# Hybrid decoder layer: key transposes one projection earlier, score matmuls of a head grouped by shape

## The chip, the cores and the metric

The kernel runs on one core of one Trainium2 chip. The metric is the device time of one execution in microseconds; less is better. The time before is the median of three executions.

## The reference

One layer on a sequence of 512 tokens of width 1024, all in float32: a layer norm, one large projection, two causal token mixers in parallel, an output projection with a second layer norm, and then a mixer that picks 16 of 16384 experts per head for every token. The change lies in the first token mixer, a gated linear recurrence that is computed in chunks (8 heads, key and value width 128):

```python
def hgrn2_mixer(q, f_logit, i, g, lb, norm_g):
    f = lb + (1.0 - lb) * jax.nn.sigmoid(f_logit.astype(f32))
    k = 1.0 - f
    logf = jnp.log(f)
    ...
    bh = jnp.cumsum(heads(logf, HG_DK), axis=3)
    q_dec = qh * jnp.exp(bh)
    k_inv = kh * jnp.exp(-bh)
    scores = jnp.where(causal, jnp.einsum('bhncd,bhnsd->bhncs', q_dec, k_inv), 0.0)
    o_intra = jnp.einsum('bhncs,bhnse->bhnce', scores, vh)
    k_end = kh * jnp.exp(b_last - bh)
    d_state = jnp.einsum('bhncd,bhnce->nbhde', k_end, vh)
    ...
    _, s_in = lax.scan(step, s0, (chunk_decay, d_state))
    o_inter = jnp.einsum('bhncd,nbhde->bhnce', q_dec, s_in)
```

So a head needs scores (decayed queries against keys), a product of the scores with the values, and a product of transposed decayed keys with the values that moves the state from one block of tokens to the next.

## The kernel before, in words

Tokens lie in four blocks of 128. Every projection is a feature tile, `proj` (line 374): 8 slices of the width times 3 matmuls of 128x128 on 128x512 (lines 123 to 125; each float32 weight is split into a high and a low part), that is 24 matmuls into one of two PSUM tiles `fp`. Its weight tile is loaded by DMA (`wraw`), its high part is cast on ACT (`wh`, line 118) and its low part subtracted on POOL (`wl`, line 119), three to four tiles ahead.

The list `slots` (lines 557 to 561) holds 44 projections. The first 24 are three for each head: the forget gate (`f_tile`), the query (`q_tile`) and the output gate (`g_tile`). Behind each projection the loop at line 562 issues parts of earlier heads. With h the head, and slot 3h the one of its `f_tile`:

- `att1(h)` behind slot 3h+3, the f projection of the next head. It transposes the decayed keys `kb` of the head (line 447, tile `k` in the trace, since the buffer is reused) into the PSUM tile `pk`, copies that to `ktok` on ACT (line 449), and computes the scores into the PSUM tile `psc`. For each of the four blocks there are four matmuls: one 128x128 (line 453), one with 64 columns of weights for the later half block against the earlier (line 455), and two with 32 columns at column positions 0 and 64 (line 459). They overwrite parts of what the first wrote, and DVE copies the result under the causal mask to `sc` (line 463).
- `att2(h)` behind slot 3h+4, the q projection of the next head. Three matmuls of `ktok` with the values (line 474, tile `pd`), and from them the states `st` on DVE (lines 475 and 477).
- `att3(h)` behind slot 3h+5, the g projection of the next head. Scores times values and queries times state (lines 487 and 489, tile `po`), squares and a norm on ACT (lines 494 to 496), a product on DVE (line 498).
- `att4(h)` behind slot 3h+7. Transposes of the result (line 506, tile `pr`), gate and split (line 508 on).

TensorE (PE) runs in the order in which the program is written. In this part the order of ACT, DVE, POOL and SyncE comes from the framework's scheduler. A PE instruction that waits for another engine holds all PE work behind it. The temporary tiles (`f`, `k`, `kinv`, `half`, `q`, `ktok`, `o`) share 15 buffers in turn, and the PSUM tiles `pk`, `psc`, `pd`, `po` and `pr` share six banks in turn.

After the mixers come the branch projection, the output projection and the norm, the expert queries with their top-16 lists, and a long phase over all 128 tiles of expert keys and values (lines 1046 to 1094).

Of the kernel before, what the change touches and what calls it, by code (L numbers as in the profile page):

```python
# [20 lines left out]
NB = 4  # L21
# [30 lines left out]
def hybrid_block(ctx, tc, ins, out, dbg=None):  # L52
# [14 lines left out]
    def bank(name="bank"):  # L67
        return psw.tile([128, 512], FT, name=name, tag="bank")
# [167 lines left out]
    with ExitStack() as pa:  # L236
# [6 lines left out]
        def tmp(name="tmp", dt=FT):  # L243
            return t2.tile([128, S], dt, name=name, tag="t2")
# [134 lines left out]
        hd = [dict() for _ in range(H)]  # L379
# [60 lines left out]
        def head(h):  # L440
            return vtok[h // 4], slice((h % 4) * 128, (h % 4 + 1) * 128)

        def att1(h):
            x = hd[h]
            pk = bank("pk")
            for blk in range(NB):
                nc.tensor.transpose(pk[:, blk * 128:(blk + 1) * 128], x["kb"][:, blk * 128:(blk + 1) * 128], ident)
            ktok = tmp("ktok")
            nc.scalar.copy(ktok, pk)
            psc_ = bank("psc")  # L450
            for blk in range(NB):
                sl = slice(blk * 128, (blk + 1) * 128)
                nc.tensor.matmul(psc_[:, sl], x["kinv"][:, sl], x["q"][:, sl], start=True, stop=True,
                                 skip_group_check=True)
                nc.tensor.matmul(psc_[0:64, blk * 128 + 64:(blk + 1) * 128], x["half"][:, 0, blk, :], x["half"][:, 1, blk, :],
                                 start=True, stop=True, skip_group_check=True)
                for j in (0, 2):
                    s = blk * 128 + j * CH
                    nc.tensor.matmul(psc_[j * CH:(j + 1) * CH, s + CH:s + 2 * CH], x["be"][:, s:s + CH],
                                     x["q"][:, s + CH:s + 2 * CH], start=True, stop=True, skip_group_check=True,  # L460
                                     tile_position=(0, j * CH))
            sc = scT[h % 2]
            nc.vector.copy_predicated(sc, smask[:, None, :].to_broadcast([128, NB, 128]),
                                      psc_.rearrange("p (b c) -> p b c", b=NB))
            x.update(ktok=ktok, sc=sc)

        def att2(h):
            x = hd[h]
# [92 lines left out]
                  (pool_tile, 3)] + [(gb_tile, t) for t in range(4, 8)] + [(ga_tile, t) for t in range(8)]  # L561
        for n, (fn, arg) in enumerate(slots):
            fn(arg)
            for lag, att in ((7, att4), (5, att3), (4, att2), (3, att1)):
                h, r = divmod(n - lag, 3)
                if r == 0 and 0 <= h < H:
                    att(h)
# [565 lines left out]
def build(nc, arrays, dbg=None):  # L1133
    ins = {k: nc.dram_tensor(f"in_{k}_dram", v.shape, mybir.dt.from_np(v.dtype), kind="ExternalInput").ap()
           for k, v in arrays.items()}
    out = nc.dram_tensor("out_0_dram", (S, D), FT, kind="ExternalOutput").ap()
    d = {k: nc.dram_tensor(f"dbg_{k}", shp, FT, kind="ExternalOutput").ap() for k, shp in (dbg or {}).items()}
    with tile.TileContext(nc) as tc:
        hybrid_block(tc, ins, out, d)
# [11 lines left out]
```

## Time and profile before

| | us |
|---|---|
| median of 3 executions (lowest to highest) | 1815.38 (1810.57 to 1819.29) |
| the profiled execution, own time | 1821.71 |
| its span in the trace | 1820.0 |
| PE busy in the span | 1759.8 |
| DVE busy | 1302.0 |
| ACT busy | 748.4 |
| POOL busy | 642.0 |

The trace shows one execution with every instruction. A float32 matmul stands in it as two records, here called passes; a transpose has one. "Busy" on PE is modelled from starts and shapes, so the distance from one start to the next tells more of its pace than the length of a record does. PEld are the weight loads, which can run beside matmuls. A time in square brackets is idle time of the engine just before the instruction, with the instruction that ended it.

### The profile page before, as it was taken

What the parts mean: (1) busy time and instruction counts of PE and PEld (TensorE: products, weight loads), DVE (VectorE), ACT (ScalarE), POOL (GpSimd) and SP (SyncE); (2) the same over time, 40 slices, a digit from 0 to 9 for tenths busy, and PEclk for the clock granted to TensorE, in tenths of its full rate; (3) what the DMA queues carried; (4) which work ended last, traced back from release to release, by engine and by line L of the source; (5) the groups of instructions that cost most, each with busy time, mean ns of one, the idle gap of its engine ahead of it and who ended that gap; (6) DMA issues with size and microseconds to landing.
All of it is one profiled execution on the core that took longest, in us unless ns stands there. A gap on an engine that the chain in (4) does not pass through costs nothing.

```text
span 1820.0 us, 25277 instructions
## 1 busy us (share of the span) xinstructions
PE 1759.8 (97%) x9677; PEld 1539.9 (85%) x9677; DVE 1302.0 (72%) x2332; ACT 748.4 (41%) x1052; POOL 642.0 (35%) x421
## 2 busy tenths in 40 slices
PE   7999999999999999999999999999999999999997
PEld 5777787888788998888988888888878888888886
DVE  6455444234589869999846887887867887878887
ACT  3567754332332355655653343323333332333332
POOL 3532323344345540000012543453433443444450
PEclk9999999999999999999999999999999999999999
DMA  4322222342233335565688999899998999899983
GB/s 145 117 69 70 60 69 87 104 139 93 77 96 115 106 109 174 197 232 192 239 291 277 367 335 375 320 317 360 315 325 291 339 336 323 312 338 325 328 304 105
DMA packets 159694, 399.10 MB, mean 219 GB/s; under 512 B 12882, under 2 KB 75858, under 8 KB 156372
## 3 DMA queue, kind: packets, MB, share of 16 engines
q1 hardware_dynamic: 115220, 253.02, 41.5%
q0 software_dynamic: 36864, 134.23, 20.5%
q10 hardware_dynamic: 7488, 10.23, 1.5%
q8 instruction: 76, 1.25, 0.3%
q14 instruction: 46, 0.38, 0.1%
HBM read 359.94 MB, written 37.49 MB: 218 GB/s over the span
## 4 chain that ended last, share of the span: by engine, by line
PE 77%; DVE 9%; DMA 5%; issue 2%; ACT 2%; ACTq 0%; DVEq 0%; SPq 0%
PE fp L123 14%; PE fp L124 14%; PE fp L125 14%; PE yacc L124 8%; PE yacc L125 8%; PE yacc L123 8%; DMA wraw<-in_v_tab_dram 4%; PE ple L841 3%; DVE A L876 2%; DVE wl L220 2%; PE pG L890 2%; DVE oh L870 2%; DMA wraw<-in_u_tab_t_dram 1%; PE sc L785 1%; PE acc L125 1%
## 5 line engine op out<-in xcount | busy, mean ns | idle before, releaser
L123 PE MATMUL fp<-othi,wh 128*128 128x384 f32 (+1 forms) x1216 | 429.2, 353 | 0.3 <-ACT othi L136 0.3
L125 PE MATMUL fp<-othi,wl 128*128 128x384 f32 (+1 forms) x1216 | 420.7, 346 | 6.2 <-DVE wl L220 6.2
L219 ACT CAST wh<-wraw 128x1024 fp32r<-128x1024 f32 x280 | 294.3, 1052 | 308.1 <-DMA wraw<-in_v_tab_dram 203.9
L124 PE MATMUL fp<-otlo,wh 128*128 128x384 f32 (+1 forms) x1216 | 419.6, 345 | 0.2 <-DVE otlo L137 0.2
L220 DVE TENSOR_TENSOR wl<-wraw,wh 128x1024 fp32r<-128x1024 f32 x246 | 300.4, 1224 | 156.1 <-ACT wh L219 155.6
L967 POOL DMA_INDIRECT rows<-in_u_tab_dram,eidx x128 | 179.6, 1403 | 494.4 <-DVE oh L870 248.3
L123 PE MATMUL yacc<-wh,ah 128*128 128x512 f32 x768 | 301.0, 392 | 6.6 <-ACT wh L219 6.6
L124 PE MATMUL yacc<-wl,ah 128*128 128x512 f32 x768 | 302.6, 394 | 4.0 <-DVE wl L220 4.0
L125 PE MATMUL yacc<-wh,al 128*128 128x512 f32 x768 | 302.0, 393 | 0.0
L967 POOL DMA_INDIRECT rows<-in_v_tab_dram,eidx x128 | 186.9, 1461 | 231.1 <-DVE hres L981 193.3
L119 POOL TENSOR_TENSOR wl<-wraw,wh 128x1024 fp32r<-128x1024 f32 x68 | 167.8, 2471 | 277.3 <-ACT wh L118 277.3
L125 PEld LDWEIGHTS fp<-othi,wl 128*128 128x128 f32 x1216 | 229.4, 189 | 14.4 <-DVE wl L220 6.9
L124 PEld LDWEIGHTS fp<-otlo,wh 128*128 128x128 f32 x1216 | 229.8, 189 | 10.3 <-DVE otlo L137 0.5
L123 PEld LDWEIGHTS fp<-othi,wh 128*128 128x128 f32 x1216 | 229.6, 189 | 10.3 <-ACT othi L136 0.5
L627 ACT ACTIVATE ge<-fp 128x384 f32<-128x384 f32 x128 | 62.9, 492 | 352.8 <-PE fp L125 352.8
L123 PEld LDWEIGHTS yacc<-wh,ah 128*128 128x128 f32 x768 | 145.2, 189 | 36.8 <-ACT wh L219 8.1
L124 PEld LDWEIGHTS yacc<-wl,ah 128*128 128x128 f32 x768 | 145.2, 189 | 35.2 <-DVE wl L220 6.2
L125 PEld LDWEIGHTS yacc<-wh,al 128*128 128x128 f32 x768 | 145.2, 189 | 30.7 <-DVE al L119 0.3
L981 DVE SCALAR_TENSOR_TENSOR hres<-rows,ggate,hres 128x1024 f32<-128x1024 f32 x128 | 164.1, 1282 | 2.4
L978 DVE SCALAR_TENSOR_TENSOR rows<-rows,hg 128x1024 f32<-128x1024 f32 x128 | 151.1, 1219 | 0.7 <-DMA rows<-in_u_tab_dram,eidx 0.7
L123 PE MATMUL fp<-xthi,wh 128*128 128x512 f32 x352 | 142.4, 405 | 1.5 <-DVE q L426 1.5
L118 ACT CAST wh<-wraw 128x1024 fp32r<-128x1024 f32 x68 | 71.1, 1048 | 163.9 <-issue 100.6
(245 smaller groups left out, 2519.5 us busy)
## 6 DMA issues: line engine op xcount, KB each, us to landing
wraw<-in_u_tab_t_dram SPq DMA_DIRECT2D x128, 512.0 KB, 4.9
wraw<-in_v_tab_dram SPq DMA_DIRECT2D x128, 512.0 KB, 7.0
Gd<-stg SPq DMA_DIRECT2D x24, 1024.0 KB, 6.3
gt<-Gd SPq DMA_DIRECT2D x16, 1536.0 KB, 15.5
wraw<-in_w_in_dram SPq DMA_DIRECT2D x44, 512.0 KB, 3.5
Hs<-ge ACTq DMA_DIRECT2D x52, 192.0 KB, 2.7
ge<-Hs SPq DMA_DIRECT2D x52, 192.0 KB, 7.5
wraw<-in_w_query_dram SPq DMA_DIRECT2D x16, 512.0 KB, 3.4
```

Source lines behind the costliest of these rows:

```text
L118: nc.scalar.copy(hi, src)
L119: lo_eng.tensor_sub(lo, src, hi.bitcast(FT))
L123: nc.tensor.matmul(o, a[0], b[0], start=start, stop=False)
L124: nc.tensor.matmul(o, a[0], b[1], start=False, stop=False)
L125: nc.tensor.matmul(o, a[1], b[0], start=False, stop=stop)
L219: f(hi, raw)
L220: g(lo, raw, hi.bitcast(FT))
L627: nc.scalar.activation(ge, p[:, :ND], AF.Gelu)
L841: nc.tensor.matmul(o, a[x], b[y], start=(cc == 0 and blk % 2 == 0 and n == 0), stop=(cc == NCK - 1 and n == 2), skip_group_check=True)
L967: nc.gpsimd.indirect_dma_start(out=r, out_offset=None, in_=ins["v_tab" if kind else "u_tab"], in_offset=bass.IndirectOffsetOnAxis(ap=eidx[ ...
L978: nc.vector.scalar_tensor_tensor(r, r, 1.0, hg[:, b, :], op0=OP.mult, op1=OP.mult, accum_out=hdot[:, b, k:k + 1])
L981: nc.vector.scalar_tensor_tensor(hres[:, b, :], r, ggate[:, b, k:k + 1], hres[:, b, :], op0=OP.mult, op1=OP.add)
```

## The change

The transposes of the keys and their copy to `ktok` leave `att1` for a function of their own, `att0`, which is issued behind slot 3h+2, the g projection of the same head: one projection earlier than before. In `att1` the matmuls of the four blocks are issued by shape: four of 128x128, four with 64 columns, four with 32 columns at position 0, four at position 64. Number, shapes and operands of all instructions stay. In the changed kernel the lines behind the new function are 4 to 6 higher: 453, 455, 459, 463, 474 and 475 are 457, 460, 465, 469, 480 and 481 there.

```diff
--- before.py
+++ after.py
@@ -440,21 +440,27 @@
         def head(h):
             return vtok[h // 4], slice((h % 4) * 128, (h % 4 + 1) * 128)
 
-        def att1(h):
+        def att0(h):
             x = hd[h]
             pk = bank("pk")
             for blk in range(NB):
                 nc.tensor.transpose(pk[:, blk * 128:(blk + 1) * 128], x["kb"][:, blk * 128:(blk + 1) * 128], ident)
             ktok = tmp("ktok")
             nc.scalar.copy(ktok, pk)
+            x["ktok"] = ktok
+
+        def att1(h):
+            x = hd[h]
             psc_ = bank("psc")
             for blk in range(NB):
                 sl = slice(blk * 128, (blk + 1) * 128)
                 nc.tensor.matmul(psc_[:, sl], x["kinv"][:, sl], x["q"][:, sl], start=True, stop=True,
                                  skip_group_check=True)
+            for blk in range(NB):
                 nc.tensor.matmul(psc_[0:64, blk * 128 + 64:(blk + 1) * 128], x["half"][:, 0, blk, :], x["half"][:, 1, blk, :],
                                  start=True, stop=True, skip_group_check=True)
-                for j in (0, 2):
+            for j in (0, 2):
+                for blk in range(NB):
                     s = blk * 128 + j * CH
                     nc.tensor.matmul(psc_[j * CH:(j + 1) * CH, s + CH:s + 2 * CH], x["be"][:, s:s + CH],
                                      x["q"][:, s + CH:s + 2 * CH], start=True, stop=True, skip_group_check=True,
@@ -462,7 +468,7 @@
             sc = scT[h % 2]
             nc.vector.copy_predicated(sc, smask[:, None, :].to_broadcast([128, NB, 128]),
                                       psc_.rearrange("p (b c) -> p b c", b=NB))
-            x.update(ktok=ktok, sc=sc)
+            x["sc"] = sc
 
         def att2(h):
             x = hd[h]
@@ -561,7 +567,7 @@
                   (pool_tile, 3)] + [(gb_tile, t) for t in range(4, 8)] + [(ga_tile, t) for t in range(8)]
         for n, (fn, arg) in enumerate(slots):
             fn(arg)
-            for lag, att in ((7, att4), (5, att3), (4, att2), (3, att1)):
+            for lag, att in ((7, att4), (5, att3), (4, att2), (3, att1), (2, att0)):
                 h, r = divmod(n - lag, 3)
                 if r == 0 and 0 <= h < H:
                     att(h)
```

TensorE, from the end of a head's output product to the first projection behind its next score block (`pk`: transposes, `psc`: scores, `po`: output, `fp`: projection). Before:

```order
L489 MATMUL po<-st,bh 128x128
L123 MATMUL fp<-xthi,wh 128x512
...
L447 MATMUL pk<-ident,k 128x128 x4
L453 MATMUL psc<-q,kinv 128x128
L455 MATMUL psc<-half 64x64
L459 MATMUL psc<-q,f 32x32 x2
...
L123 MATMUL fp<-xthi,wh 128x512
```

The three score rows stand there four times, once for each block. With the change:

```order
L495 MATMUL po<-st,bh 128x128
L447 MATMUL pk<-ident,k 128x128 x4
L123 MATMUL fp<-xthi,wh 128x512
...
L457 MATMUL psc<-q,kinv 128x128 x4
L460 MATMUL psc<-half 64x64 x4
L465 MATMUL psc<-q,f 32x32 x8
L123 MATMUL fp<-xthi,wh 128x512
```

The transposes now stand ahead of the 24 matmuls of the next f projection, and the scores change shape three times from one projection to the next.

ScalarE (ACT), from the cast behind the exponentials of a head to the cast behind the norm (`wh`: weight cast, `q` and `sg`: gates of projections, `ss`: norm). Before:

```order
L118 CAST wh<-wraw 128x1024
L449 COPY ktok<-pk 128x512
L425 ACT_TABLE_LOAD
L425 ACTIVATE q<-fp 128x512
...
L436 ACTIVATE sg<-fp 128x512
L494 ACTIVATE o_1006,ss<-po 128x128 x4
L495 ACT_TABLE_LOAD
```

With the change:

```order
L118 CAST wh<-wraw 128x1024
L425 ACT_TABLE_LOAD
L425 ACTIVATE q<-fp 128x512
...
L436 ACTIVATE sg<-fp 128x512
L500 ACTIVATE o_1006,ss<-po 128x128 x4
L449 COPY ktok<-pk 128x512
L501 ACT_TABLE_LOAD
```

The copy leaves its place behind a head's weight cast and stands one projection earlier, between the squares and the norm of the head before.

VectorE (DVE), from the keys of a head to the states of the head before (`f`, `k`, `half`: decayed keys, `st`: states). Before:

```order
L410 TENSOR_TENSOR f<-f,k 128x512
L418 TENSOR_TENSOR k<-f,dtab_381 128x512
L418 TENSOR_TENSOR half<-f,dtab_381 128x256
L508 SCALAR_TENSOR_TENSOR o<-pr,ng,sg 128x512
L475 COPY st<-pd 128x128
```

With the change:

```order
L410 TENSOR_TENSOR f<-f,k 128x512
L481 COPY st<-pd 128x128
L418 TENSOR_TENSOR k<-f,dtab_381 128x512
L418 TENSOR_TENSOR half<-f,dtab_381 128x256
L514 SCALAR_TENSOR_TENSOR o<-pr,ng,sg 128x512
```

The first copy of the state, which needs `pd` from PE, moves ahead of the decayed keys `k` that the transposes read. Beside these places DVE moves the mask copy by one or two rows in the first and the last head; the orders of POOL and SyncE are the same in both kernels.

## Rows read from the trace of the kernel before

**Rows 1.** The page, part 1: busy us, share of the span, records of each engine.

```profile
PE 1759.8 (97%) x9677; PEld 1539.9 (85%) x9677; DVE 1302.0 (72%) x2332; ACT 748.4 (41%) x1052; POOL 642.0 (35%) x421
```

**Rows 2.** By stretch: busy us (records) of PE, PEld, DVE, ACT, POOL; clock, DMA share, GB/s.

```profile
91.00:265.00 174.00, 166.46 (x956) 136.38 (x954) 86.44 (x168) 123.95 (x218) 53.41 (x22) 1.00 0.21 67
265.00:320.00 55.00, 55.00 (x252) 44.03 (x251) 27.31 (x49) 20.22 (x32) 19.45 (x8) 1.00 0.25 82
...
1200.00:1600.00 400.00, 391.55 (x1890) 345.27 (x1889) 314.42 (x392) 133.64 (x188) 173.65 (x124) 0.99 0.94 326
```

**Rows 3.** Waits of all engines in 91 to 265 us: in total, times, longest (us).

```profile
PEld pd L474 <- ACT ktok L449: 9.4, 7, 1.9
...
PE pd L474 <- ACT ktok L449: 7.5, 7, 1.4
```

**Rows 4.** PE in order of time, one head: start, us (both us), engine, line, operation.

```profile
115.95 0.60 PE L447 MATMUL pk<-ident,k 128*128 128x128 f32 x4
116.38 0.39 PE L453 MATMUL psc<-q,kinv 128*128 128x128 f32 x2
116.70 0.33 PE L455 MATMUL psc<-half 128*64 128x64 f32 x2
116.96 0.25 PE L459 MATMUL psc<-q,f 128*32 128x32 f32 x4
117.14 0.49 PE L453 MATMUL psc<-q,kinv 128*128 128x128 f32 x2
...
119.73 0.50 PE L123 MATMUL fp<-xthi,wh 128*128 128x512 f32 x1
120.06 0.39 PE L124 MATMUL fp<-xtlo,wh 128*128 128x512 f32 x1
120.29 0.40 PE L125 MATMUL fp<-xthi,wl 128*128 128x512 f32 x1
...
125.31 0.60 PE L506 MATMUL pr<-ident,o 128*128 128x128 f32 x4
126.92 0.94 PE L474 MATMUL pd<-vtok,ktok 128*128 128x128 f32 x6 [1.02 <-ACT ktok L449]
...
133.19 0.61 PE L487 MATMUL po<-vtok,scT 128*128 128x128 f32 x4
```

**Rows 5.** The second L455 pass alone (shorter stretch); three weight loads (PEld) of the transposes.

```profile
116.80 0.22 PE L455 MATMUL psc<-half 128*64 128x64 f32 x1
...
115.95 0.36 PEld L447 LDWEIGHTS pk<-ident,k 128*128 128x128 f32 x3
```

**Rows 6.** Score matmuls grouped by line and shape: busy us, mean ns of one record.

```profile
L453 PE MATMUL psc<-q,kinv 128*128 128x128 f32 x64 | 14.8, 313 | 0.0
...
L459 PE MATMUL psc<-q,f 128*32 128x32 f32 x128 | 8.2, 206 | 0.0
```

**Rows 7.** ACT in order of time, around the copy of the transposed keys.

```profile
115.96 1.04 ACT L118 CAST wh<-wraw 128x1024 fp32r<-128x1024 f32 x1 [1.02 <-issue]
...
121.50 0.63 ACT L388 ACTIVATE f<-f 128x512 f32<-128x512 f32 x1 [1.29 <-DVE k L387]
...
126.29 0.58 ACT L449 COPY ktok<-pk 128x512 f32<-128x512 f32 x1
```

**Rows 8.** DVE in order of time, same stretch: normalised output, decayed keys, state.

```profile
114.97 0.69 DVE L498 TENSOR_TENSOR o<-po,ss 128x512 f32<-128x512 f32 x1 [3.78 <-ACT ss L496]
...
125.07 0.69 DVE L410 TENSOR_TENSOR f<-f,k 128x512 f32<-128x512 f32 x1
125.79 0.69 DVE L418 TENSOR_TENSOR k<-f,dtab 128x512 f32<-128x512 f32 x1
...
127.89 0.29 DVE L475 COPY st<-pd 128x128 f32<-128x128 f32 x1 [0.41 <-PE pd L474]
```

**Rows 9.** First head: its decayed keys on DVE, and the wait of PE before the second head.

```profile
84.44 0.69 DVE L418 TENSOR_TENSOR k<-f,dtab 128x512 f32<-128x512 f32 x1
...
86.14 0.50 PE L123 MATMUL fp<-xthi,wh 128*128 128x512 f32 x1 [1.48 <-DVE q L426]
```

**Rows 10.** The chain that ended last, from 320 us on: its last piece before the weighted phase.

```profile
943.46 12.29 DMA gt<-Gd
```


## The prediction

> **What bounds the kernel now.** The page's part 1 comes first: PE is busy 97% of the span [rows 1]. Then the table by stretch shows what that hides. In 91 to 265 us, where the eight heads run, PE is busy 166.46 of 174 us; behind it, in 265 to 320 us, it never pauses; from 1200 to 1600 us the DMA engines are 94% busy [rows 2]. So in the stretch that the change touches PE sets the pace and is short of full by 7.5 us. The waits of that stretch name the gap: one wait by `pd` on the ACT copy `ktok`, seven times, 7.5 us on PE and 9.4 us if counted at the weight load [rows 3]. PE in order of time shows the rest: a head comes every 24.3 us, and its scores are short matmuls whose starts lie far apart [rows 4]. The reader is to see two losses per head: a hole of 1 us, and a block of scores that costs twice its columns. The granted clock there is 1.00, that is 2.4 GHz [rows 2], and both kernels have the same passes, so no clock enters the sum.
>
> **Term 1, the wait for `ktok`.** The four `pr` transposes start at 125.31 and take 4 x 0.108 us (from 115.95 to 116.38 the same four take 0.43), so `pd` could start at 125.74; it starts at 126.92, 1.18 late, and its first weight load, 0.10, is no longer hidden [rows 4]. The copy that ended the wait ran on ACT at 126.29 [rows 7], though its transposes were done ten microseconds before: it stood in ACT's queue behind the exponentials and a weight cast. With the change the copy runs one projection earlier, and nothing else that `pd` needs is late: the values are long there. Six heads at 1.28 and one longer wait make the 9.4 us of the weight load's row; the lower end is PE's own 7.5 [rows 3]. I take **9.4 us**, since each wait exposes its load. The eighth head had no wait.
>
> **Term 2, the scores by shape.** First the present cost, from starts [rows 4]. The first 128x128 pair lasts 0.32 us up to the 64-column pair: 2 passes at 0.108 and 0.10 over. The 64-column pair lasts 0.26: its second pass starts 0.10 behind its first [rows 5], which is one load and one pass of 0.054, half of 0.108; then a second pass and again 0.10 over. The 32-column four last 0.18: load 0.027, two steps of 0.027 with both positions side by side, and 0.10 over. The next block begins 0.76 after the first began, but the three later blocks take (119.73 - 117.14) / 3 = 0.86: back at 128 columns a load of 0.10 is exposed too. At the end the first projection matmul lasts 0.33 to the next start, against 0.23 normally, 0.10 more. So each change of shape costs 0.10 us and an exposed load, twelve times a head. All together: 119.73 - 116.38 + 0.10 = 3.45 us.
>
> Now the new block has three changes of shape. Eight 128-column passes at 0.108: 0.87, and 0.10. Eight 64-column passes: one load 0.054 and 8 x 0.054, then 0.10: 0.59. Sixteen 32-column passes: load 0.027 and 16 x 0.027, then 0.10: 0.56. The projection's load: 0.10. Sum 2.22, so 1.23 us less per head. The trace has 64 records of line 453, eight for each of eight heads [rows 6]; 8 x 1.23 = **9.8 us**.
>
> The step with no row is the long run of 32-column passes at one position. Before, two positions alternate and share their time; by shape they stand four and four. I charge 16 steps of 0.027 instead of 8, 0.22 us a head, which is already in the sum. The upper end is that no sharing is lost: 8 x 1.45 = 11.6 us. The lower end is that within a group no pass hides its load: 0.43 more on the 64-column group and 0.43 on the 32-column group leave 0.37 a head, 3.0 us. I take the middle value because it is nearest to the transposes, the only long run of one shape: three of their weight loads lie in 0.36 us, and their starts are 0.108 apart [rows 4, 5], so there the loads are hidden. That points away from the lower end. The Trainium skill (TensorE: Matmul & The Clock Gate, Part 3, "What overlaps and what doesn't") says that a weight load overlaps a matmul in flight only where their row groups differ. All these matmuls use all rows; by that rule term 2 would be the lower end, and the transposes of this trace disagree with it.
>
> **Term 3, the moved transposes.** Four transposes of 0.43 us go from one place on PE to another, eight times; the shape before and behind them is 128x128 in either place, so seven of them cost what they cost. The first head's fall into a hole: PE waits 1.48 us there until 86.14, and the keys are ready at 84.44 + 0.69 = 85.13 [rows 9], so its transposes fit into the wait: **0.4 us** saved, with nothing lost at worst.
>
> **What must stay hidden.** The copy of 0.58 us now stands ahead of the norm on ACT. Behind the norm ACT idles 1.02 us before its next weight cast [rows 7], which covers it; without that cover the cast would be 0.6 late, and it feeds a tile several projections away. DVE's product `o` would end 0.6 later than 115.66 [rows 8], and PE reads it at 125.31 [rows 4]. On DVE the first state copy now stands ahead of the keys `k`. PE ends `pd` some 2.5 us earlier, and ACT no longer waits 1.29 us for DVE [rows 7], since the score mask before that comes earlier; so the exponentials and the line 410 product, which end at 125.76, move about as far. I expect the copy to hold DVE for about 1 us, and `k` to end near the present 126.48 [rows 8]. The transposes would read it behind `po`: today that begins at 133.19 and takes 1.5, so at 134.7, less 2.5 gained, 132.2. Slack: over 5 us. No DMA issue moves past another one, since the orders of SyncE and POOL are the same. PSUM banks and the 15 buffers are used in turn at the same distance as before, and each old reader is done at least a slot earlier.
>
> **The sum.** 9.4 + 9.8 + 0.4 = 19.6 us, all on PE. The chain reaches the weighted phase by way of a load at 943.46 us that waits for all that came before [rows 10], so an earlier start should last to the end. The profiled execution took 1821.7, that is 6.3 more than the median of 1815.4; by its trace 1802.1, and by the median **1795.8 us**, 1.1% faster. About 0.5% (9.1 us) is what a measurement of this kernel can tell from no change.
>
> **The rivals.**
> - *Loads stay exposed in the groups.* Term 2 is 3.0 us: 12.8 gained, 1802.6. For it: the 64-column pair shows one exposed load. Against it: that is the load behind a change of shape, and the transposes hide theirs. If the group gained nothing at all, the wait alone would give 1815.4 - 9.8 = 1805.6.
> - *The gain is given back later.* The DMA engines are 94% busy from 1200 us on [rows 2]. If the transfers there do not begin earlier, PE waits for them instead: 1811 to 1815. Against it: the first of them waits for work that PE now ends earlier.
> - *The change does not do what it says.* The framework orders ACT; had it left the copy behind the cast, the wait would stay and only term 2 come, 1805. The order shows the copy moved, so this has almost no weight.
> - *The transposes become the wait: slower.* PE takes them in order, ahead of the f projection. `k` stands behind the state copy on DVE, that waits for `pd` on PE, and so a late DVE would hold all of PE, once a head. The gain is 2.5 us a head; the kernel turns slower by 0.5% when each wait passes (19.6 + 9.1) / 8 = 3.6 us, so when `k` is 5 + 3.6, some 9 us later than I reckon. At 5 us a head: 1815.4 - 19.6 + 40 = 1836. Against it: DVE is busy 86 of 174 us here [rows 2].
>
> **How the numbers follow.** Forecast 0.70; loads exposed or no gain by shape 0.16; given back later 0.09; transposes wait 0.03; copy not moved 0.02. The forecast's own range is 1790 to 1802: the terms' ends 7.5 + 9.8 and 9.4 + 11.6, give or take the 4.4 us by which the three runs scatter. The range reaches on to the cases of one term, 1788 to 1808, and leaves out less than 2 in 10. Faster by over 0.5% means under 1806.3: the forecast and nearly all of the one-term cases, 0.85. Slower 0.03, and 0.12 between.
>
> **What would show it.** Right: no wait of `pd` on `ktok`; the distance from the first 453 to the projection about 2.1 us; heads 21.8 us apart; PE full between 91 and 250 us. Term 2 is wrong if the 32-column starts lie 0.05 apart. All of it is wrong if PE waits at the transposes, or if the chain's waits for value tiles grow by what the heads gave.

## The result, and the profile after

| | before | changed |
|---|---|---|
| median of 4 executions, us | 1816.44 | 1798.77 |
| lowest to highest | 1810.57 to 1819.29 | 1788.79 to 1800.53 |
| profiled execution: span | 1820.0 | 1798.8 |

The kernel before has one execution more here than in the table above. The ratio is 0.989 with a 95% interval of 0.986 to 0.992: faster by 1.1%, by 17.7 us between the medians and 21.2 us between the spans. The forecast was 1795.8, with 1790 to 1802 as its own range.

First the busy time of the engines from the page, the stretch of the heads and a late one (columns as in [rows 2]), and the waits by PE and by ACT's `f` in 85 to 265 us, of the changed kernel:

```profile
PE 1750.0 (97%) x9677; PEld 1537.9 (85%) x9677; DVE 1327.0 (74%) x2332; ACT 749.4 (42%) x1052; POOL 644.5 (36%) x421
```

```profile
91.00:265.00 174.00, 174.00 (x1053) 148.24 (x1052) 122.59 (x189) 132.98 (x235) 60.69 (x24) 1.00 0.25 76
...
1200.00:1600.00 400.00, 392.44 (x1889) 346.25 (x1887) 311.47 (x381) 131.66 (x185) 169.08 (x122) 0.99 0.96 330
```

```profile
ACT f L388 <- DVE k L387: 1.9, 1, 1.9
...
PE pk L447 <- DVE k L418: 0.5, 1, 0.5
...
PE fp L123 <- DVE q L426: 0.3, 1, 0.3
```

PE is now busy for all 174 us, where 7.5 us were missing [rows 2]. The wait of `pd` on `ktok` [rows 3] has no row any more. What is left are two short waits of the first head. One head on PE in order of time:

```profile
107.22 0.60 PE L447 MATMUL pk<-ident,k 128*128 128x128 f32 x4
...
113.13 1.05 PE L457 MATMUL psc<-q,kinv 128*128 128x128 f32 x8
114.11 0.68 PE L460 MATMUL psc<-half 128*64 128x64 f32 x8
114.72 0.59 PE L465 MATMUL psc<-q,f 128*32 128x32 f32 x16
115.24 0.50 PE L123 MATMUL fp<-xthi,wh 128*128 128x512 f32 x1
...
120.82 0.60 PE L512 MATMUL pr<-ident,o 128*128 128x128 f32 x4
121.26 0.83 PE L480 MATMUL pd<-vtok,ktok 128*128 128x128 f32 x6
...
128.94 0.60 PE L447 MATMUL pk<-ident,k 128*128 128x128 f32 x4
...
134.86 1.05 PE L457 MATMUL psc<-q,kinv 128*128 128x128 f32 x8
```

`pd` follows `pr` at 0.44 us instead of 1.61 [rows 4], with no bracket. The scores begin at 113.13 and the projection behind them at 115.24: 2.11 us instead of 3.35. From one head's scores to the next it is 21.73 us; before it was 24.25.

To see whether the gain lasts, take two fixed places: the first projection matmul of the first head, and the line 109 product of the second layer norm that takes 3.32 us, the only one so long. PE and DVE in order of time, before:

```profile
68.18 0.39 PE L123 MATMUL fp<-xthi,wh 128*128 128x512 f32 x1
...
465.82 3.32 DVE L109 SCALAR_TENSOR_TENSOR hres<-hres,ln_mv,gb 128x1024 f32<-128x1024 f32 x1
```

After:

```profile
68.25 0.39 PE L123 MATMUL fp<-xthi,wh 128*128 128x512 f32 x1
...
446.14 3.32 DVE L109 SCALAR_TENSOR_TENSOR hres<-hres,ln_mv,gb 128x1024 f32<-128x1024 f32 x1
```

The chain that ended last, of the changed kernel, at the load that begins the weighted phase:

```profile
925.59 12.28 DMA gt<-Gd
```

Between them lie 397.64 us before and 377.89 after: **19.75 us less**, against 19.6 forecast. The load begins 17.9 us earlier than at 943.46 [rows 10]; that this is 1.9 us less than 19.75 lies within the scatter of the late phase. From the line 109 product to the end both kernels issue the same instructions in the same order; they took 1354.2 and 1352.7 us there, and in the six experiments below between 1345.9 and 1355.8. That scatter is why the whole time tells the gain only roughly (the interval of the ratio stands for 14.5 to 26 us), and why I read the experiments by these two places first.

### The profile page after: what moved, and what is told of

It reads as the page before. It is cut to its first block, busy times and chain, and to the rows that moved or that the text cites. A ratio compares the mean times of both kernels' runs of the same rounds, so it can differ in the third digit from the quotient of the medians.

```text
span 1798.8 us, 25265 instructions
## 1 busy us (share of the span) xinstructions
PE 1750.0 (97%) x9677; PEld 1537.9 (85%) x9677; DVE 1327.0 (74%) x2332; ACT 749.4 (42%) x1052; POOL 644.5 (36%) x421
## 4 chain that ended last, share of the span: by engine, by line
PE 82%; DVE 8%; DMA 6%; issue 2%; ACT 1%; SPq 0%; POOL 0%; ACTq 0%; DVEq 0%; POOLq 0%
PE fp L123 15%; PE fp L125 15%; PE fp L124 15%; PE yacc L124 8%; PE yacc L125 8%; PE yacc L123 8%; DMA wraw<-in_v_tab_dram 3%; PE ple L847 3%; PE pG L896 2%; DVE A L882 2%; DVE wl L220 2%; PE acc L124 1%; PE acc L125 1%; PE acc L123 1%; DVE oh L876 1%
## 5 line engine op out<-in xcount | busy, mean ns | idle before, releaser
L219 ACT CAST wh<-wraw 128x1024 fp32r<-128x1024 f32 x280 | 294.3, 1053 | 300.5 <-DMA wraw<-in_v_tab_dram 192.6
L125 PE MATMUL fp<-xthi,wl 128*128 128x512 f32 x352 | 137.3, 390 | 0.0
```

Of the source, the lines that this page charges most:

```text
L125: nc.tensor.matmul(o, a[1], b[0], start=False, stop=stop)
L219: f(hi, raw)
```

## The experiments

| kernel | median, us | ratio to before (95%) | head to head | between the two places |
|---|---|---|---|---|
| before | 1816.44 | | 24.25 | 397.64 |
| the change | 1798.77 | 0.989 (0.986 to 0.992) | 21.73 | 377.89 |
| 1: only the move | 1807.08 | 0.993 (0.991 to 0.996) | 22.95 | 387.67 |
| 2: only the grouping | 1809.56 | 0.995 (0.994 to 0.997) | 23.03 | 387.89 |
| 3: positions alternate | 1799.99 | 0.991 (0.989 to 0.993) | 21.58 | 376.74 |
| 4: groups of two blocks | 1807.54, one run | | 22.07 | 380.70 |
| 5: two projections ahead | 1812.14 | 0.998 (0.995 to 1.000) | 22.92 | 393.89 |
| 6: 64 columns cut in two | 1796.07 | 0.989 (0.986 to 0.993) | 21.45 | 375.62 |

Each ratio is to runs of the kernel before on the same chip, whose medians were 1816.98 (1 to 4) and 1817.85 (5 and 6).

### 1. Only the move

The score loop is put back to its old order, block by block:

```diff
             for blk in range(NB):
                 sl = slice(blk * 128, (blk + 1) * 128)
                 nc.tensor.matmul(psc_[:, sl], ...
-            for blk in range(NB):
                 nc.tensor.matmul(psc_[0:64, ...
-            for j in (0, 2):
-                for blk in range(NB):
+                for j in (0, 2):
                     s = blk * 128 + j * CH
```

> Only the transposes and their copy are moved; the scores keep their old order by block. Theory (two separate losses on PE, which add): the wait of pd on ktok is gone and the first head's transposes fall into its hole, so 9.8 us less than before, about 1806; heads 23.0 us apart (24.3 less 1.3); the score block still 3.45 us long. Rival (the regrouping makes all the gain, the copy was hidden anyway): no change, heads 24.3 us apart. Rival (the move makes all the gain by relieving ACT): the whole 19.7 us, heads 21.7 us apart.

A head takes 22.95 us, 1.30 less than before, and 10.0 us are gone between the two places. The waits in 85 to 265 us:

```profile
ACT f L388 <- DVE k L387: 6.9, 7, 1.9
```

No row of a `pd` that waits for ACT is left, and PE has only the first head's waits of 0.5 and 0.3 us. The score block still takes 3.34 us. ACT itself still waits for DVE seven times, so what counted was the place of the copy, and not a less busy ACT. Both rivals fall.

### 2. Only the grouping

The kernel before, with the three score loops of the change:

```diff
                 nc.tensor.matmul(psc_[:, sl], ...
+            for blk in range(NB):
                 nc.tensor.matmul(psc_[0:64, ...
-                for j in (0, 2):
+            for j in (0, 2):
+                for blk in range(NB):
                     s = blk * 128 + j * CH
```

> Only the scores are grouped by shape; transposes and copy stay behind the f projection. Theory (ACT's chain to the copy is itself held by the score mask on DVE, by the 1.29 us that ACT waits for DVE, so it moves ahead with the scores): the wait of pd stays near 1.1 us a head, the score block falls to 2.2 us, heads 23.0 us apart, about 9.8 us less than before. Rival (ACT's chain has its own time, counted from the f projection): pd waits 2.3 us a head and eats the whole gain, heads 24.3 us apart, no change.

The waits in 85 to 265 us, first one of the kernel before, then those of this one:

```profile
ACT f L388 <- DVE k L387: 9.2, 7, 1.4
```

```profile
PEld pd L476 <- ACT ktok L449: 9.3, 7, 1.9
...
PE pd L476 <- ACT ktok L449: 7.4, 7, 1.4
...
ACT f L388 <- DVE k L387: 1.4, 1, 1.4
```

A head takes 23.03 us, 1.22 less, and the wait of `pd` stays as it was, 7.4 us. PE did not simply come earlier to a copy as late as before: the mask on DVE came earlier, ACT's seven waits for DVE (one of them the 1.29 us in [rows 7]) shrank to one, and the copy moved ahead with the scores. In both kernels it starts 6.6 us behind the first projection matmul that follows the scores. So the two losses are separate: 9.97 and 9.75 us between the two places for the parts, 19.75 for both.

### 3. The two positions alternate

```diff
-            for j in (0, 2):
-                for blk in range(NB):
+            for blk in range(NB):
+                for j in (0, 2):
```

> The changed kernel, but the 32-column matmuls alternate between positions 0 and 64, block after block, as before. Theory (two positions run side by side, a long run at one position cannot): the 32-column group falls from 0.56 to 0.34 us, 0.22 us a head, 1.7 us in all against the changed kernel, which is visible in the trace and below what the times can tell. Rival (the start-to-start distance is a floor of the queue, whatever the position): the group stays at 0.56.

```profile
110.63 1.05 PE L457 MATMUL psc<-q,kinv 128*128 128x128 f32 x8
111.61 0.68 PE L460 MATMUL psc<-half 128*64 128x64 f32 x8
112.22 0.45 PE L465 MATMUL psc<-q,f 128*32 128x32 f32 x16
112.59 0.50 PE L123 MATMUL fp<-xthi,wh 128*128 128x512 f32 x1
```

From the first 32-column start to the projection it is 0.37 us, in the changed kernel 115.24 - 114.72 = 0.52. Side by side is faster, as the theory has it, but by 0.15 a head instead of 0.22: 1.2 us in all. The single starts in the traces tell why it is less. In the changed kernel position 64 does not wait for the end of position 0: its first pass starts 0.15 us behind the first at position 0, with the fifth of eight. Here the two positions start 0.01 us apart.

### 4. Groups of two blocks

```diff
+            for two in ((0, 1), (2, 3)):
-            for blk in range(NB):
+                for blk in two:
```

The other two loops run over `two` in the same way, inside the new one.

> The changed kernel, but grouped by shape in two pairs of blocks: six changes of shape a head instead of three. Theory (each change costs 0.10 us and the load behind it): 3 x 0.10 + 0.054 + 0.027 + 0.108 = 0.49 us more a head, score block 2.7 us, 3.9 us more in all than the changed kernel. Rival (the gain comes from shape groups of a certain length, or from the order in which banks are written, not from the number of changes): the block keeps 2.2 us or goes back to 3.4.

```profile
114.57 0.60 PE L458 MATMUL psc<-q,kinv 128*128 128x128 f32 x4
115.10 0.45 PE L461 MATMUL psc<-half 128*64 128x64 f32 x4
115.48 0.33 PE L466 MATMUL psc<-q,f 128*32 128x32 f32 x8
115.73 0.71 PE L458 MATMUL psc<-q,kinv 128*128 128x128 f32 x4
116.38 0.45 PE L461 MATMUL psc<-half 128*64 128x64 f32 x4
116.75 0.33 PE L466 MATMUL psc<-q,f 128*32 128x32 f32 x8
117.01 0.50 PE L123 MATMUL fp<-xthi,wh 128*128 128x512 f32 x1
```

The block takes 2.44 us, between the 2.11 of one group and the 3.35 of four: the number of changes counts, so the rivals fall, but the added cost is 0.33 a head and not 0.49 (2.8 us in all between the two places, where 3.9 was expected). Group by group: the two 128-column groups last 0.53 + 0.65 = 1.18 against 0.98 in the changed kernel, 0.20 more, as reckoned (0.21). The 64-column groups last 0.38 + 0.37 = 0.75 against 0.61, 0.14 more (0.15). The 32-column groups last 0.25 + 0.26 = 0.51 against 0.52: nothing, where 0.13 was reckoned. With runs of two matmuls at one position the next position starts 0.01 us behind and runs beside it all the way. The miss is the same as in experiment 3, seen from the other side.

### 5. Two projections ahead

```diff
-            for lag, att in ((7, att4), (5, att3), (4, att2), (3, att1), (2, att0)):
+            for lag, att in ((7, att4), (5, att3), (4, att2), (3, att1), (1, att0)):
```

> The changed kernel, but the transposes are moved two projections ahead instead of one: behind the q projection of the same head. Theory (the rival of the prediction made to happen: transposes that come before their keys hold all of PE): the first head waits from 79.4 us to about 85.2 us, of which 0.8 us were waits in the changed kernel, so some 4.9 us are lost; each later head waits for the keys about 1.2 us, since on DVE they stand behind the first state copy; heads 22.9 us apart; 13 us more than the changed kernel, about 1812. Rival (earlier is better or the same, ACT gets more air): no wait at the transposes, about 1799.

The waits of PE in 78 to 265 us, and a later head:

```profile
PEld pk L447 <- DVE k L418: 14.9, 8, 6.3
...
PE pk L447 <- DVE k L418: 13.1, 8, 5.9
```

```profile
130.80 0.66 PE L447 MATMUL pk<-ident,k 128*128 128x128 f32 x4 [0.98 <-DVE k L418]
```

Every head now waits for its keys; 16.0 of the 19.75 us are given back between the two places, and the ratio of 0.998 is just below no change. That is more than the 9.97 us that the move had brought: against experiment 2, which moves nothing, the stretch is 6.0 us longer. So the rival in which the transposes become the wait is real, and one projection lies between it and the change. Later heads lost 1.19 us each, as reckoned. The first lost more than its wait. Stretches of this kernel around it (columns as in [rows 2]):

```profile
84.00:88.00 4.00, 3.86 (x11) 3.23 (x12) 2.81 (x6) 0.95 (x2) 0.00 (x0) 0.50 0.14 55
88.00:92.00 4.00, 4.00 (x16) 3.20 (x15) 0.00 (x0) 0.00 (x0) 0.00 (x0) 0.82 0.00 0
92.00:98.00 6.00, 6.00 (x28) 4.96 (x27) 0.69 (x1) 1.54 (x2) 2.39 (x1) 1.00 0.13 32
```

Behind 5.89 us of idle PE the granted clock was 0.50, the 1.2 GHz level, and the projection began at half pace: its records lie 0.43 us apart up to 89.3 us, where 0.23 is normal. The first head's scores came 7.25 us later than in the changed kernel, counted from the first place, where 4.9 were reckoned; some ten matmuls 0.2 us late each are most of the rest. In the changed kernel the first head's waits are 0.53 and 0.30 us, and the clock there is 1.00.

### 6. The 64-column matmuls cut in two

On top of experiment 3:

```diff
             for blk in range(NB):
-                nc.tensor.matmul(psc_[0:64, blk * 128 + 64:(blk + 1) * 128], x["half"][:, 0, blk, :], x["half"][:, 1, blk, :],
-                                 start=True, stop=True, skip_group_check=True)
+                for r in (0, CH):
+                    nc.tensor.matmul(psc_[r:r + CH, blk * 128 + 64:(blk + 1) * 128], x["half"][:, 0, blk, r:r + CH],
+                                     x["half"][:, 1, blk, :], start=True, stop=True, skip_group_check=True,
+                                     tile_position=(0, r))
```

> The alternating kernel of the third experiment, with each 64-column score matmul cut into two of 32 columns at positions 0 and 32: one change of shape less a head, twice the matmuls there. Theory (each change costs 0.10 us and its load, positions run side by side): the block falls from 1.97 by 0.10 + 0.05 to about 1.8 us, 1.2 us in all, far below what the times can tell. Rival (twice the matmuls cost twice the time): the 32-column part of the old 64-column group takes 0.47 us more, block 2.3 us.

```profile
113.07 1.05 PE L457 MATMUL psc<-q,kinv 128*128 128x128 f32 x8
114.05 0.58 PE L461 MATMUL psc<-half 128*32 128x64 f32 x13
114.42 0.22 PE L467 MATMUL psc<-q,f 128*32 128x32 f32 x1
114.42 0.27 PE L461 MATMUL psc<-half 128*32 128x64 f32 x2
114.47 0.20 PE L467 MATMUL psc<-q,f 128*32 128x32 f32 x1
114.47 0.22 PE L461 MATMUL psc<-half 128*32 128x64 f32 x1
114.52 0.41 PE L467 MATMUL psc<-q,f 128*32 128x32 f32 x14
114.87 0.50 PE L123 MATMUL fp<-xthi,wh 128*128 128x512 f32 x1
```

1.80 us for the block, as reckoned. The 0.10 is gone where line 467 follows line 461: operands and streamed columns (64, then 32) change there, and only the weights keep their 32 columns. So the 0.10 goes with the width of the weights, and not with a change of operands. Between the two places it is the shortest of all, 375.62 us, 2.3 less than the changed kernel. Its median, 1796.07, can't be told from 1798.77.

## Why the prediction was right

**The bound.** That PE sets the pace in the heads, and that its holes and its changes of shape are what can be saved, is shown: the head distance fell by 2.52 us, from 24.25 to 21.73, and experiments 1 and 2 give 1.30 and 1.22 of it.

**Term 1 with term 3, 9.8 us.** Experiment 1 measured 9.97. The choice of the weight load's 9.4 over PE's own 7.5 was right: each wait had cost 1.18 in `pd`'s start and 0.10 in an exposed load. The first head of the changed kernel:

```profile
85.26 0.66 PE L447 MATMUL pk<-ident,k 128*128 128x128 f32 x4 [0.53 <-DVE k L418]
86.22 0.50 PE L123 MATMUL fp<-xthi,wh 128*128 128x512 f32 x1 [0.30 <-DVE q L426]
```

Its transposes stand in the hole that ended at 86.14 before [rows 9], and the next projection starts at 86.22, though its transposes are already done: 0.4 us, as said.

**Term 2, 9.8 us.** Experiment 2 measured 9.75. The block of 2.11 plus the projection's exposed 0.10 is the 2.22 that was reckoned, but two parts of it were mis-sized and cancel. The 64-column group lasts 0.61 instead of 0.59: behind the second pass the starts lie 0.058 us apart in the trace, a little more than half of 0.108. The 32-column group lasts 0.52 instead of 0.56: the step that had no row, sixteen single steps at 0.027, failed. The steps at one position are longer, 0.032 us, and the second position runs partly beside the first; experiments 3 and 4 show both sides of it. The sign of a wrong term, 32-column starts 0.05 us apart, stood only between the first and the second pass of each position. That the total came out is in this part luck: a sum that fits is no proof of its terms.

**Hidden loads.** The lower end, 3.0 us, needed exposed loads within a group. The loads (PEld) of one head's first group in the changed kernel:

```profile
112.91 1.08 PEld L457 LDWEIGHTS psc<-q,kinv 128*128 128x128 f32 x8
114.11 0.54 PEld L460 LDWEIGHTS psc<-half 128*64 128x64 f32 x8
```

Eight loads in 1.08 us, while the eight passes start over 0.98: the loads lie beside the matmuls. The rule of the Trainium skill that the prediction weighed (TensorE: Matmul & The Clock Gate, Part 3, "What overlaps and what doesn't") does not hold for these matmuls, which all use all rows.

**Covers.** ACT, DVE and POOL of the changed kernel, from the cast behind the norm to the keys:

```profile
113.15 1.04 ACT L118 CAST wh<-wraw 128x1024 fp32r<-128x1024 f32 x1 [0.98 <-issue]
...
122.13 0.29 DVE L481 COPY st<-pd 128x128 f32<-128x128 f32 x1 [0.45 <-PE pd L480]
...
122.33 0.68 DVE L418 TENSOR_TENSOR k<-f,dtab 128x512 f32<-128x512 f32 x1
...
122.39 2.88 POOL L119 TENSOR_TENSOR wl<-wraw,wh 128x1024 fp32r<-128x1024 f32 x1 [5.74 <-ACT wh L118]
...
122.93 2.62 DVE L418 TENSOR_TENSOR half<-f,dtab 128x256 f32<-128x256 f32 x1
```

Ahead of that cast ACT still idles 0.98 us, with the copy now before the norm, so the copy delayed nothing there. The state copy held DVE for 0.65 us, 0.45 of them waiting (about 1 was said), the keys ended at 123.01 and the transposes read them at 128.94: 5.9 us of slack, where over 5 was said. The two times themselves were forecast as 126.48 and 132.2, each some 3.4 us too late, in the main because the gains of the heads before were not all taken off; both moved alike, so the slack came out. Experiment 5 shows what happens without it. That the gain would last to the end is shown as far as the scatter of the late phase lets it: from the second norm on the two kernels differ by 1.5 us.

## What to carry to other kernels

On an engine that runs in program order, a short matmul that waits for a copy can be helped by moving the copy's source one stage earlier, and the next late operand tells how far: here one projection was worth 10 us, and a second one cost 16 us, more than the first had brought. Short matmuls of different column widths are best counted by their starts: each change of the weights' width cost 0.10 us and a bare weight load here, so group by width, and within a width alternate the column positions. Where two parts of a change act on one engine, run each alone: the sum told that they add, and the groups told that two of the prices were wrong.

## What was not expected

- **A DVE product of 0.42 us took 2.6.** In the rows just above, `half` is 128x256 and took 0.42 before (eight, mean 418 ns, and 2072 ns in the changed kernel). It starts 0.5 us into POOL's subtract of 2.88 us and ends 0.28 us behind it. DVE's busy time over the whole span rose from 1302.0 [rows 1] to 1327.0 us with the same 2332 records. In experiment 1 it is `k` that is held and `half` takes 0.41, in experiment 2 neither, so it goes by who begins while POOL works: of the 256 products of line 418 in the traces of the eight kernels, the 71 that begin inside such a subtract take 2.50 to 2.90 us, and all others 0.41 to 0.69. The kernel before has one of the 71. The Trainium skill (GPSIMD Engine Reference, 1. Specifications) says that GpSimd shares its SBUF interfaces with VectorE and that VectorE instructions with two SBUF inputs contend; the trace agrees, with these numbers. No experiment took the subtract away. Here PE covered it; with less slack, such a hold of `k` could make the transposes wait, which no run shows.
- **Matmuls at different positions start out of program order.** In experiment 6 all matmuls of line 461 stand ahead of those of line 467, yet one of 467 starts at 114.42 with three of 461 still to start. So PE does not keep the program's order to the letter: these starts fit one that holds for each position by itself.
- **Behind one wait the clock was halved.** 5.89 us of idle PE in experiment 5 were followed by matmuls at the 0.50 level, and the first head lost 2.3 us more than reckoned.
